# Up projection of forty column pairs as seven half-size products each, down projection as two sweeps over eight banks

## The chip, the cores and the metric

One core of a Trainium2 chip runs the whole program. The metric is device time in microseconds (us) of one execution. Five engines work side by side, each through its own queue in order: TensorE (PE; PEld is its weight load), VectorE (DVE), ScalarE (ACT), GpSimd (POOL) and SyncE (SP), which issues the DMAs. SBUF is the on-chip memory of 128 partitions, PSUM has eight banks of 128 x 512 float32, into which PE accumulates.

## What is computed

A decoder block for 512 tokens of width 2048: modulated RMS norm, a mixer, a residual, a second modulated norm, and the gated MLP that this case is about, with D_FF = 5632:

```python
h = _rmsnorm(x, norm2_g[l]) * (1.0 + sc2) + sh2
x = x + gt2 * _conv_ffn(h, w_up[l], conv_w[l], conv_b[l], w_down[l])
...
u = h @ w_up
up = jnp.pad(u, ((0, 0), (CONV_WIDTH - 1, 0), (0, 0)))
y = conv_b
for j in range(CONV_WIDTH):
    y = y + conv_w[j] * up[:, j:j + T]
val, gate = jnp.split(y, 2, axis=-1)
return (jax.nn.silu(gate) * val) @ w_down
```

The convolution runs over tokens, three taps per column. A final RMS norm ends the program. Everything is float32.

## The kernel before, in words

Activations lie transposed, columns on partitions and the 512 tokens along the free axis. A matrix product of float32 accuracy is made of three matmuls: weights and activations are each split into a high part (a cast to fp32r on ACT) and a low part (the rest, a subtraction on DVE), and `mm3` (L115 to L118) issues high x high (L116), high weights x low activations (L117) and low x high (L118). `split_weights` (L105 to L113) loads 128 x 512 weights into `wraw` (four buffers), casts them to `whi` on ACT (L110) and subtracts to `wlo` (L112, on DVE, or on POOL where a caller says so); `whi` and `wlo` have three buffers each. `project` runs a column tile's k-tiles through it, four at a time.

The program has a first part up to about 815 us (gates, input projection, mixers) that the change leaves as it is. Then, in the pool `rb`:

- The output projection, with the residual `x2` in 16 SBUF tiles and the sum of squares for the second norm. Its last columns are made by token halves, so that the norm of one half can begin early.
- `second_norm` (L144 to L146) writes the MLP's input H2, 16 tiles in high and low parts. `up_first` makes the first four column tiles by token halves, 256 tokens at a time, 16 k-tiles each; in the pass of the first half every other low part is made on POOL.
- A pair is the value tile j and the gate tile j, 44 pairs in all. `up_tile` makes one tile with 48 matmuls of 512 columns; `conv` applies the three taps (ACT at L896, DVE at L897 and L898, all of which read the bank), ACT does the Silu (L908), DVE the product (L909), and `split_act` the split into high and low (L138, L139).
- Pairs come in six groups (8, 8, 8, 8, 4, 8). After each group its part of the down projection runs: for each of the 16 output tiles the group's k-tiles into one bank, added to `x2` under the gate by DVE at L924. The last group does the final residual, the norm and the stores, its last eight tiles by token halves.
- `ada_gate2` computes the MLP's output gate, which needs 64 loads of 256 KB and 64 operations of DVE (L886); they are put behind pairs 4 to 7.

The order within an engine's queue is set by a scheduler with its own estimates of durations, from the order in which the code is written and from the buffers; queues are not reordered at run time.

## Time and profile before

| | |
|---|---|
| median of 3 runs | 2382.52 us (2381.91 to 2382.76) |
| the profiled execution's own time | 2381.72 us |
| its span in the trace | 2379.9 us |
| mean granted clock of PE | 0.979 |
| DVE busy, ACT busy, POOL busy | 1354.4 us, 821.2 us, 27.1 us |
| DMA | 357.06 MB, mean 150 GB/s |
| up-projection weights, down-projection weights | 368 and 192 loads of 256 KB |

The page gives, for each engine, its busy time, the chain of work that ended last, and groups of instructions by line with the mean duration of one and the idle time before them. Matmuls are pipelined, so the duration drawn for one is longer than the distance to the next; the distance is what counts. Lines are those of the program above, with L in front.

### The profile page before, as it was taken

Reading aid. Unit: us, or ns where it says so; the run is one execution under the profiler, and the core shown is the slowest. Engines: PE = TensorE matmul, PEld = TensorE weight load, DVE = VectorE, ACT = ScalarE, POOL = GpSimd, SP = SyncE. Lnnn points to the kernel's source line nnn. Section 1 sums busy time; section 2 is a strip of 40 time slices with the busy share of each in tenths; the row PEclk is TensorE's granted clock in tenths of the full one; section 3 lists DMA queues with packets and bytes.
Section 4 is the critical chain, followed back from the end, with each engine's and each line's share of the span. In section 5 each row is a group of like instructions: output and inputs, shape, how many; then the busy total and the mean of one; then the engine's idle time right before and its main releaser. Section 6 shows DMA issues by size and latency. Waiting matters only on the chain.

```text
span 2379.9 us, 36912 instructions
## 1 busy us (share of the span) xinstructions
PE 2258.0 (95%) x14434; PEld 1828.4 (77%) x14434; DVE 1354.4 (57%) x2258; ACT 821.2 (35%) x1361; POOL 27.1 (1%) x30
## 2 busy tenths in 40 slices
PE   7998898899879899999999999999999999999997
PEld 5776656666566799877888888888888888888886
DVE  7897767575875467577344433444344434444457
...
GB/s 350 296 301 168 171 178 182 185 124 215 219 232 149 182 173 207 104 224 223 97 97 96 96 98 98 98 98 94 97 97 98 98 97 97 95 97 98 98 101 174
DMA packets 188226, 357.06 MB, mean 150 GB/s; under 512 B 36497, under 2 KB 48529, under 8 KB 183825
## 3 DMA queue, kind: packets, MB, share of 16 engines
...
q8 instruction: 113, 1.85, 0.3%
...
HBM read 336.25 MB, written 18.36 MB: 149 GB/s over the span
## 4 chain that ended last, share of the span: by engine, by line
PE 76%; DMA 11%; DVE 7%; issue 3%; ACT 2%; SPq 1%; DVEq 0%; POOL 0%; ACTq 0%
PE b L116 20%; PE b L118 20%; PE b L117 20%; DMA war<-ada 4%; PE mm L118 2%; PE mm L117 2%; PE mm L116 2%; PE pf L116 2%; PE pf L118 2%; PE pf L117 2%; DMA wa<-ada 1%; DVE war L367 1%; DMA slot<-ada 1%; DVE wlo L112 1%; DMA wraw<-wup 1%
## 5 line engine op out<-in xcount | busy, mean ns | idle before, releaser
L112 DVE TENSOR_TENSOR wlo<-wraw,whi 128x512 fp32r<-128x512 f32 (+1 forms) x786 | 534.6, 682 | 664.8 <-ACT whi L110 650.1
L110 ACT CAST whi<-wraw 128x512 fp32r<-128x512 f32 (+1 forms) x802 | 490.9, 614 | 1222.2 <-PE b L117 918.4
L118 PE MATMUL b<-hh,wlo 128*128 128x512 f32 (+1 forms) x1472 | 560.9, 381 | 5.8 <-DVE wlo L112 5.5
L116 PE MATMUL b<-hh,whi 128*128 128x512 f32 (+1 forms) x1472 | 560.0, 380 | 0.8 <-ACT whi L110 0.8
L117 PE MATMUL b<-hl,whi 128*128 128x512 f32 (+1 forms) x1472 | 559.5, 380 | 0.0
L116 PE MATMUL b<-ah,whi 128*128 128x512 f32 (+1 forms) x980 | 350.3, 358 | 5.2 <-ACT whi L110 3.7
L118 PE MATMUL b<-ah,wlo 128*128 128x512 f32 (+1 forms) x980 | 349.3, 357 | 4.2 <-DVE wlo L112 4.2
L117 PE MATMUL b<-al,whi 128*128 128x512 f32 (+1 forms) x980 | 348.9, 356 | 0.0
L118 PEld LDWEIGHTS b<-hh,wlo 128*128 128x128 f32 x1472 | 277.0, 188 | 61.8 <-DVE wlo L112 8.2
L116 PEld LDWEIGHTS b<-hh,whi 128*128 128x128 f32 x1472 | 276.9, 188 | 53.1 <-ACT whi L110 1.4
L117 PEld LDWEIGHTS b<-hl,whi 128*128 128x128 f32 x1472 | 276.9, 188 | 52.7
L116 PEld LDWEIGHTS b<-ah,whi 128*128 128x128 f32 x980 | 186.4, 190 | 34.9 <-ACT whi L110 6.1
L118 PEld LDWEIGHTS b<-ah,wlo 128*128 128x128 f32 x980 | 186.3, 190 | 31.1 <-DVE wlo L112 5.3
L117 PEld LDWEIGHTS b<-al,whi 128*128 128x128 f32 x980 | 186.4, 190 | 26.8 <-DVE al L139 1.2
L118 PE MATMUL mm<-ah,wlo 128*128 128x512 f32 x444 | 187.6, 423 | 5.9 <-DVE wlo L112 5.8
L116 PE MATMUL mm<-ah,whi 128*128 128x512 f32 x444 | 186.6, 420 | 6.4 <-ACT whi L110 6.3
L117 PE MATMUL mm<-al,whi 128*128 128x512 f32 x444 | 184.9, 416 | 0.0
L367 DVE SCALAR_TENSOR_TENSOR war<-war,cq 128x1024 f32<-128x1024 f32 x96 | 117.2, 1222 | 83.2 <-DMA war<-ada 82.5
L924 DVE SCALAR_TENSOR_TENSOR x<-b,mod,x 128x512 f32<-128x512 f32 x80 | 59.7, 750 | 111.7 <-PE b L118 111.7
L116 PE MATMUL pf<-ah,whi 128*128 128x512 f32 x256 | 95.9, 404 | 20.6 <-ACT ah L214 19.5
L116 PEld LDWEIGHTS mm<-ah,whi 128*128 128x128 f32 x444 | 87.4, 197 | 32.0 <-ACT whi L110 8.1
L118 PEld LDWEIGHTS mm<-ah,wlo 128*128 128x128 f32 x444 | 87.2, 196 | 30.2 <-DVE wlo L112 8.4
...
## 6 DMA issues: line engine op xcount, KB each, us to landing
wraw<-wup SPq DMA_DIRECT2D x368, 256.0 KB, 3.0
...
wraw<-wdn SPq DMA_DIRECT2D x192, 256.0 KB, 2.7
...
```

What stands on the lines that cost most here:

```text
L110: S.copy(hi[:, 0:w], raw[:, 0:w])
L112: eng.tensor_tensor(lo[:, 0:w], raw[:, 0:w], hi[:, 0:w].bitcast(F32), op=ALU.subtract)
L116: PE.matmul(ps, wh, xh, start=start, stop=False)
L117: PE.matmul(ps, wh, xl, start=False, stop=False)
L118: return PE.matmul(ps, wl, xh, start=False, stop=stop)
L367: V.scalar_tensor_tensor(wa, wa, 1.0, cq[0], op0=ALU.mult, op1=ALU.mult, accum_out=modq[:, kq, j : j + 1])
L924: V.scalar_tensor_tensor(x2[f], ps, mod[:, 80 + f : 81 + f], x2[f], op0=ALU.mult, op1=ALU.add)
```

## The change

Pairs 0 to 3 stay as they were. For pairs 4 to 43 a pair's product is seen as a 2 x 2 block product: two halves of the 16 k-tiles by (gate, value) columns, times two halves of the tokens. It is computed with seven products of half the k-tiles and half the tokens in place of eight, from sums of weight quarters and sums of token quarters. The token sums are made once, on POOL (`token_sums`), cast on ACT and split on DVE, and lie in the slots `ah`, `al`. The weight sums are made per pair in four chunks (`seven`): one load of 512 KB brings four quarters of two k-tiles, POOL makes four sums, ACT and DVE split three quarters and four sums. The seven results stay in seven banks and are combined by ACT and DVE into `cv` and `cg`, in SBUF, which `conv` then reads. The packing of the weights on the host follows (`wups`), without arithmetic.

All 44 activation products are stored to DRAM (`actd`), and `x2` too (`x2d`). The down projection runs after all pairs, in two sweeps of eight output tiles, one bank each, over all 44 k-tiles in groups of four; the activations are loaded and split again in each sweep. The second sweep keeps its last eight k-tiles for the token halves. The loads and operations of `ada_gate2` are spread two to a pair over pairs 4 to 35.

```diff
-GROUPS = (8, 8, 8, 8, 4, 8)
+NORD = 4
+NPC = 4
+DK = 4
...
+    def gated(j, cv, cg):
+        yv, yg = conv(cv, j, "t0"), conv(cg, 44 + j, "t1")
+        S.activation(yg, yg, AF.Silu)
+        after = V.tensor_mul(yv, yv, yg)
+        nc.sync.dma_start(actd[j], yv)
+        return after
...
+    for j in range(2):
+        gated(j, ups[2 * j], ups[2 * j + 1])
...
+    def token_sums(i):
+        bb = up.tile([P, 2, T], F32, tag="raw", name="bb", bufs=3)
+        for q in range(2):
+            hi, lo = H2[i + HK * q]
+            G.tensor_tensor(bb[:, q, :], hi[:, :].bitcast(F32), lo[:, :].bitcast(F32), op=ALU.add)
+        tt = up.tile([P, 2, T], F32, tag="raw", name="tt", bufs=3)
+        t1, t2, t3, t4 = (tt[:, q // 2, (q % 2) * HT : (q % 2 + 1) * HT] for q in range(4))
+        G.tensor_tensor(t1, bb[:, 0, HT:], bb[:, 0, 0:HT], op=ALU.subtract)
+        G.tensor_tensor(t3, bb[:, 1, HT:], bb[:, 0, 0:HT], op=ALU.subtract)
+        G.tensor_tensor(t2, bb[:, 1, HT:], t1, op=ALU.subtract)
+        G.tensor_tensor(t4, t2, bb[:, 1, 0:HT], op=ALU.subtract)
+        got = []
+        for q in range(2):
+            hi, lo = slot(2 * i + q), slot(16 + 2 * i + q)
+            S.copy(hi, tt[:, q, :])
+            V.tensor_tensor(lo, tt[:, q, :], hi[:, :].bitcast(F32), op=ALU.subtract)
+            got += half([(hi, lo)], 0) + half([(hi, lo)], 1)
+        TK.append(got)
...
+    def seven(j):
+        q = {}
+        for c in range(NPC):
+            raw = up.tile([P, 4, W2], F32, tag="raw", name="raw", bufs=3)
+            nc.sync.dma_start(raw, a["wups"][j - NORD, c, :, :, :])
+            sm = [wp.tile([P, WC], F32, tag="wraw", name="sums", bufs=4) for _ in range(2)]
+            sa, sb2 = (t[:, :].rearrange("p (n w) -> p n w", n=2) for t in sm)
+            G.tensor_tensor(sa, raw[:, 1:3, :], raw[:, 0:1, :].to_broadcast([P, 2, W2]), op=ALU.add)
+            G.tensor_tensor(sb2[:, 0, :], sa[:, 0, :], raw[:, 2, :], op=ALU.add)
+            G.tensor_tensor(sb2[:, 1, :], sb2[:, 0, :], raw[:, 3, :], op=ALU.add)
...
+                    S.copy(hi[:, n : n + m, :], t)
+                    V.tensor_tensor(lo[:, n : n + m, :], t, hi[:, n : n + m, :].bitcast(F32), op=ALU.subtract)
...
+            a22, a11, a12 = parts([raw[:, 1:4, :]])
+            s1, s3, s2, s4 = parts([sa, sb2])
...
+            for n, w, xs_ in (
+                (1, a11, [x[0] for x in lo]), (2, a12, [x[1] for x in lo]),
+                (4, a22, [TK[k][3] for k in ks]), (6, s2, [TK[k][1] for k in ks]),
+                (7, s3, [TK[k][2] for k in ks]), (5, s1, [TK[k][0] for k in ks]),
+                (3, s4, [x[1] for x in hi]),
+            ):
...
+        S.copy(cg[:, A1], q[1])
+        V.tensor_tensor(cv[:, A1], cg[:, A1], q[2], op=ALU.add)
+        V.tensor_tensor(u[:, 0, :], cg[:, A1], q[6], op=ALU.subtract)
+        V.tensor_tensor(u[:, 1, :], u[:, 0, :], q[7], op=ALU.add)
+        V.tensor_tensor(u[:, 2, :], u[:, 0, :], q[5], op=ALU.subtract)
+        V.tensor_tensor(cg[:, B1], q[5], u[:, 1, :], op=ALU.subtract)
+        V.tensor_tensor(cv[:, B1], u[:, 2, :], q[3], op=ALU.add)
+        V.scalar_tensor_tensor(cg[:, A1], u[:, 1, :], -1.0, q[4], op0=ALU.mult, op1=ALU.subtract)
+        return cv, cg
...
+    for j in range(NORD, NF):
+        after = gated(j, *seven(j))
+        for n in range(2 * (j - NORD), 2 * (j - NORD + 1)):
+            if n < 4 * KT:
+                ada_gate2(n, after)
...
+    pss = [bank() for _ in range(NB)]
+    for k0 in range(0, NF, DK):
+        A = act_tiles(k0)
+        for f in range(NB):
+            down(pss[f], f, k0, DK, A, k0 == 0, k0 + DK == NF)
+            if k0 + DK == NF:
+                residual(f, pss[f], gate(f), acc, 0, T, f == 0)
```

Line numbers in the changed program: `mm3` L118 to L120, the casts and subtractions of `split_weights` L112 and L114; in `conv` and `gated` L833 to L835, L840 (Silu), L841 (product), L842 (store); the token sums L909 and L912 to L915 on POOL, L919 (cast) and L920 (subtraction); in `seven` L944 to L946 (POOL), L954 (cast), L955 (subtraction), L981 to L988 (the combination); L1002 the gate's operations.

Two places in the queues. The first is ACT at the end of `up_first`'s second pass and the start of the pairs (`whi` is a weight cast, `tk` a cast of a token sum `tt`; the number of a buffer rises with the program's order, and the casts up to whi_9739 before, whi_9818 now, are those of that pass). Before:

```order
L110 CAST whi_9703<-wraw_9701 128x512 [waits DMAHW3_49,DVE_49,PE_49]
L110 CAST whi_9721<-wraw_9719 128x512 [waits DMAHW4_49,DVE_49,PE_49]
L110 CAST whi_9739<-wraw_9737 128x512 [waits DMAHW5_49,DVE_49,PE_49]
L110 CAST whi_9795<-wraw_9793 128x512 [waits DMAHW6_49,DVE_49,PE_49]
L110 CAST whi_9813<-wraw_9811 128x512 [waits DMAHW7_49,DVE_49,PE_49]
L896 ACTIVATE t0_9764<-b_9084,vec_64 128x512 [waits PE_49]
```

With the change, from the eleventh token cast on:

```order
L919 CAST tk_9948<-tt_9943 128x512 [waits Pool_49]
L919 CAST tk_9952<-tt_9943 128x512 [waits Pool_49]
L112 CAST whi_9782<-wraw_9780 128x512 [waits DMAHW3_49,DVE_49,PE_49]
L919 CAST tk_9964<-tt_9959 128x512 [waits Pool_49]
L919 CAST tk_9968<-tt_9959 128x512 [waits Pool_49]
L112 CAST whi_9800<-wraw_9798 128x512 [waits DMAHW4_49,DVE_49,PE_49]
L919 CAST tk_9980<-tt_9975 128x512 [waits Pool_49]
L112 CAST whi_9818<-wraw_9816 128x512 [waits DMAHW5_49,DVE_49,PE_49]
L919 CAST tk_9984<-tt_9975 128x512 [waits Pool_49]
L112 CAST whi_9991<-wraw_9989 128x512 [waits DMAHW6_49,DVE_49,PE_49]
L112 CAST whi_10009<-wraw_10007 128x512 [waits DMAHW7_49,DVE_49,PE_49]
L833 ACTIVATE t0_9838<-b_9163,vec_64 128x512 [waits PE_49]
```

All 16 casts of token sums stand ahead of the first tap of pair 0, one or two between each two weight casts. Ahead of the first of them POOL has its 16 subtractions of `out_half` and `up_first`, and then the token sums, each dependent one with a wait:

```order
L114 TENSOR_TENSOR wlo_9532<-wraw_9528,whi_9530 128x512 [waits DVE_49,DMAHW5_49,PE_49,Activation_49]
L909 TENSOR_TENSOR bb_9860<-hh0_7868,hl0_7869 128x512
L909 TENSOR_TENSOR bb_9860<-hh8_7884,hl8_7885 128x512 [waits DVE_49]
L912 TENSOR_TENSOR tt_9863<-bb_9860 128x256 [waits Pool_49]
L913 TENSOR_TENSOR tt_9863<-bb_9860 128x256 [waits Pool_49]
L914 TENSOR_TENSOR tt_9863<-bb_9860,tt_9863 128x256 [waits Pool_49]
```

Before, POOL has nothing behind those 16 subtractions.

The second place is DVE in the steady part. Before, one pair of the fourth group (`t` is a tap's tile, `b` a bank):

```order
L897 SCALAR_TENSOR_TENSOR t_13901<-b,vec,t_13901 128x511
L898 SCALAR_TENSOR_TENSOR t_13901<-b,vec,t_13901 128x510
L112 TENSOR_TENSOR wlo<-wraw,whi 128x512 x4
L897 SCALAR_TENSOR_TENSOR t_13978<-b,vec,t_13978 128x511
L898 SCALAR_TENSOR_TENSOR t_13978<-b,vec,t_13978 128x510
L112 TENSOR_TENSOR wlo<-wraw,whi 128x512
L909 TENSOR_TENSOR t_13901<-t_13901,t_13978 128x512
L139 TENSOR_TENSOR al_13985<-t_13901,ah_13984 128x512
L112 TENSOR_TENSOR wlo<-wraw,whi 128x512 x3
```

With the change, the part of a pair in which the results of one pair are combined (`raw` a loaded quarter, `sums` POOL's sums, `ul` the low part, `cv`, `cg`, `u` the combination):

```order
L984 TENSOR_TENSOR u<-u,b 128x256
L985 TENSOR_TENSOR u<-u,b 128x256
L986 TENSOR_TENSOR cg<-b,u 128x256
L987 TENSOR_TENSOR cv<-u,b 128x256
L988 SCALAR_TENSOR_TENSOR cg<-u,b 128x256
L955 TENSOR_TENSOR ul<-raw,uh 128x768
L834 SCALAR_TENSOR_TENSOR t_11101<-cv,vec,t_11101 128x511
L834 SCALAR_TENSOR_TENSOR t_11105<-cg,vec,t_11105 128x511
L835 SCALAR_TENSOR_TENSOR t_11101<-cv,vec,t_11101 128x510
L835 SCALAR_TENSOR_TENSOR t_11105<-cg,vec,t_11105 128x510
L955 TENSOR_TENSOR ul<-sums,uh 128x512 x2
L841 TENSOR_TENSOR t_11101<-t_11101,t_11105 128x512
```

L982 and L983 stand ahead of these rows, each before a L955, and the two L1002 behind them. A pair has 26 operations on DVE now, 19 of them with all operands in SBUF and seven that read a bank, where it had 14; the taps read `cv` and `cg` in SBUF instead of a bank.

## Rows read from the trace of the kernel before

**Rows 1.** The page: busy times, and the chain that ended last by engine.
```profile
PE 2258.0 (95%) x14434; PEld 1828.4 (77%) x14434; DVE 1354.4 (57%) x2258; ACT 821.2 (35%) x1361; POOL 27.1 (1%) x30
...
PE 76%; DMA 11%; DVE 7%; issue 3%; ACT 2%; SPq 1%; DVEq 0%; POOL 0%; ACTq 0%
```

**Rows 2.** Stretches: us, busy PE, PEld, DVE, ACT, POOL (instructions), clock, DMA share, GB/s.
```profile
1000.00:1050.00 50.00, 49.64 (x220) 40.77 (x219) 32.40 (x67) 16.90 (x28) 0.00 (x0) 1.00 0.54 175
1050.00:1100.00 50.00, 45.17 (x188) 35.93 (x187) 39.34 (x95) 14.55 (x24) 0.00 (x0) 0.97 0.79 257
1100.00:2310.00 1210.00, 1210.00 (x5333) 999.83 (x5333) 531.05 (x786) 372.19 (x596) 0.00 (x0) 1.00 0.32 100
```

**Rows 3.** Timeline of PE in the tail: start, duration, first and last of 84.
```profile
2329.82 0.28 PE L116 MATMUL b<-ah,whi 128*128 128x256 f32 x1
...
2339.78 0.28 PE L118 MATMUL b<-ah,wlo 128*128 128x256 f32 x1
```

**Rows 4.** Groups of DVE from 860 us: count, busy us, mean ns, idle before.
```profile
L112 DVE TENSOR_TENSOR wlo<-wraw,whi 128x512 fp32r<-128x512 f32 x572 | 395.8, 693 | 586.8 <-ACT whi L110 582.5 <-PE b L117 1.1
...
L924 DVE SCALAR_TENSOR_TENSOR x<-b,mod,x 128x512 f32<-128x512 f32 x80 | 59.7, 750 | 111.7 <-PE b L118 111.7
L886 DVE SCALAR_TENSOR_TENSOR slot<-slot 128x512 f32<-128x512 f32 x64 | 42.3, 687 | 9.7 <-DMA slot<-ada 9.5
...
L144 DVE SCALAR_TENSOR_TENSOR h<-x,gsc,b 128x256 f32<-128x256 f32 x32 | 14.1, 469 | 0.0
...
L798 DVE SCALAR_TENSOR_TENSOR x<-b,mod,x 128x256 f32<-128x256 f32 x24 | 11.6, 484 | 6.8 <-PE b L118 6.3
```

**Rows 5.** Groups of ACT from 860 us.
```profile
L110 ACT CAST whi<-wraw 128x512 fp32r<-128x512 f32 x588 | 365.7, 623 | 945.1 <-PE b L117 899.6 <-DMA wraw<-wup 21.0 <-DMA wraw<-wdn 6.9
L896 ACT ACTIVATE t<-b,vec 128x512 f32<-128x512 f32 x88 | 67.8, 774 | 0.0
```

**Rows 6.** Timeline of DVE at 881 to 930, and at 1042.
```profile
881.84 0.86 DVE L144 SCALAR_TENSOR_TENSOR h<-x,gsc,b 128x256 f32<-128x256 f32 x2
...
886.54 0.48 DVE L798 SCALAR_TENSOR_TENSOR x<-b,mod,x 128x256 f32<-128x256 f32 x1 [0.27 <-PE b L118]
887.12 1.08 DVE L112 TENSOR_TENSOR wlo<-wraw,whi 128x512 fp32r<-128x512 f32 x1
...
928.40 0.48 DVE L146 SCALAR_TENSOR_TENSOR hl<-h,mod,hh 128x256 fp32r<-128x256 f32 x1
...
929.58 1.00 DVE L112 TENSOR_TENSOR wlo<-wraw,whi 128x512 fp32r<-128x512 f32 x1
...
1042.31 1.89 DVE L112 TENSOR_TENSOR wlo<-wraw,whi 128x512 fp32r<-128x512 f32 x3
```

**Rows 7.** Timeline of POOL at the same times.
```profile
886.34 1.30 POOL L112 TENSOR_TENSOR wlo<-wraw,whi 128x512 fp32r<-128x512 f32 x1 [2.21 <-DVE hl L146]
...
928.60 1.43 POOL L112 TENSOR_TENSOR wlo<-wraw,whi 128x512 fp32r<-128x512 f32 x1 [3.38 <-ACT whi L110]
```

**Rows 8.** Groups of POOL, whole span.
```profile
L112 POOL TENSOR_TENSOR wlo<-wraw,whi 128x512 fp32r<-128x512 f32 x16 | 21.0, 1310 | 304.5 <-ACT whi L110 293.8 <-DVE hl L146 8.8 <-DVE acc L791 1.9
...
L90 POOL MEMSET eps<- 128x1 f32 x1 | 0.1, 98 | 0.0
```

**Rows 9.** Timeline of ACT at the end of `up_first`'s second pass.
```profile
951.79 0.62 ACT L110 CAST whi<-wraw 128x512 fp32r<-128x512 f32 x1 [0.82 <-PE b L117]
953.23 0.62 ACT L110 CAST whi<-wraw 128x512 fp32r<-128x512 f32 x1 [0.82 <-PE b L117]
953.76 2.78 ACT L896 ACTIVATE t<-b,vec 128x512 f32<-128x512 f32 x4
```

**Rows 10.** One stretch of the first part, columns as in group 2.
```profile
820.00:840.00 20.00, 14.71 (x72) 12.16 (x71) 14.59 (x24) 9.15 (x16) 0.00 (x0) 0.74 0.71 243
```

More of the change, by code (lines that the diff above doesn't have):

```diff
@@ L776, in block_kernel, with stage @@
     HT = T // 2
+    H2 = [(rb.tile([P, T], F32R, tag=f"hh{k}", name=f"hh{k}"), rb.tile([P, T], F32R, tag=f"hl{k}", name=f"hl{k}"))
+          for k in range(KT)]
+    x2d = [tc.dram_tile([P, T], F32, name=f"x2d{f}") for f in range(KT)]
+    actd = [tc.dram_tile([P, T], F32, name=f"actd{j}") for j in range(NF)]
+    def stage(name):
+        st = ExitStack()
+        return st, st.enter_context(tc.tile_pool(name=name, bufs=1, reuse_waits="tile"))
     def bank():
@@ L865, in block_kernel @@
         up_first(1, k)
+    rxctx.close()
     if stop == "B":
         return
[L870 to L887 removed]
+    upctx, up = stage("up")
@@ L889, in up_tile @@
+    for i in range(HK):
+        token_sums(i)
     def up_tile(n):
         ps = bank()
[L891 removed]
+        project(ps, a["wup"][n - 4, :, :], H2)
         return ps
[L894 to L899 removed]
@@ new lines, in block_kernel, with ada_gate2 @@
+    cbs = []
+    modg = cp.tile([P, 4, KT], F32, tag="modg", name="modg")
+    def ada_gate2(n, after):
+        kq, j = divmod(n, KT)
+        if j == 0:
+            cbs.append(wp.tile([P, WC], F32, tag="whi", name="cb2", bufs=3))
+            nc.sync.dma_start(cbs[kq], cact[0:1, kq * T : (kq + 1) * T].partition_broadcast(P))
+        wa = wp.tile([P, WC], F32, tag="wlo", name="wa3", bufs=3)
+        nc.sync.dma_start(wa, a["ada3"][kq, j, :, :])
+        with tc.issue_after(after.ins):
+            V.scalar_tensor_tensor(wa, wa, 1.0, cbs[kq], op0=ALU.mult, op1=ALU.mult, accum_out=modg[:, kq, j : j + 1])
@@ new lines, in block_kernel, with gate, act_tiles @@
+    x2 = []
+    for f in range(KT):
+        t = rx.tile([P, T], F32, tag=f"x2_{f}", name=f"x2_{f}")
+        nc.sync.dma_start(t, x2d[f])
+        x2.append(t)
+    acc = rx.tile([P, T], F32, tag="acc", name="acc")
+    def gate(f):
+        return mod[:, 80 + f : 81 + f]
+    def act_tiles(k0):
+        got = []
+        for k in range(k0, k0 + DK):
+            t = wp.tile([P, WC], F32, tag="wraw", name="ald", bufs=4)
+            nc.sync.dma_start(t, actd[k])
+            got.append(split_act(k % KT, t))
+        return got
@@ new lines, in block_kernel @@
+    pss = [bank() for _ in range(NB)]
+    KL = NF - 2 * DK
+    for k0 in range(0, KL, DK):
+        A = act_tiles(k0)
+        for f in range(NB):
+            down(pss[f], NB + f, k0, DK, A, k0 == 0, k0 + DK == KL)
+            if k0 + DK == KL:
+                V.scalar_tensor_tensor(x2[NB + f], pss[f], gate(NB + f), x2[NB + f], op0=ALU.mult, op1=ALU.add)
+    A = act_tiles(KL) + act_tiles(KL + DK)
+    for hf in range(2):
+        for n in range(NB):
+            f = NB + n
+            if hf and n == 1:
+                dg = norm_rows(acc[:, 0:HT])
+            if hf and n == 2:
+                rstd = norm_bcast(dg)
+            if hf:
+                for k in range(max(3 * (n - 2), 0), min(3 * (n - 1), KT) if n < 7 else KT):
+                    finish(0, k, rstd)
+            ps = bank()[:, 0:HT]
+            down(ps, f, KL, 2 * DK, half(A, hf), True, True)
+            residual(f, ps, gate(f), acc, hf * HT, (hf + 1) * HT, False)
@@ L964, in pack @@
+    rstd = norm_bcast(norm_rows(acc[:, HT:T]))
+    for k in range(KT):
+        finish(1, k, rstd)
+    rxctx.close()
 def pack(x, c, w_ada, b_ada, norm1_g, w_in, mu_shift, w0, w2, a0, a2, g2, k_k, k_a, r_k, ln_x_w, ln_x_b,
```

149 lines of the change are left out of this document (61 added, 88 removed).

## The prediction

> **What bounds the kernel now.** I read the page first: TensorE is busy for 95% of the span and 76% of the chain that ended last is PE, in the three lines of `mm3` [rows 1]. Then the table of stretches [rows 2]: from 1100 to 2310 us PE is never idle, at a granted clock of 1.00, while DVE is busy for 531 of 1210 us, ACT for 372 and POOL for none. So in the stage that the change rewrites PE alone sets the time, and 1210.00 us / 5333 matmuls = 0.2269 us per 512-column matmul. The only hole of that stage is at 1050 to 1100, 50 - 45.17 = 4.8 us (and 0.4 before it), where the 64 loads of the second adaLN gate fall into five pairs and DMA stands at 0.79. Anything that the change saves must therefore be PE issue time, and anything that it adds to DVE, ACT or POOL is free only as long as these stay below PE's own time for a pair.
>
> **PE's side of the change.** A pair is now 96 matmuls of 512 columns, 96 x 0.2269 = 21.78 us; 40 pairs are 871.3 us. Seven half-size products are 7 x 8 k-tiles x 3 = 168 matmuls of 256 columns. Their price stands in the tail of this kernel: from 2329.82 to 2339.78 there are 83 steps of one 256-column matmul, 9.96 / 83 = 0.120 us each [rows 3], although each is drawn 0.28 us long. 168 x 0.120 = 20.16 us, 806.4 us for 40 pairs: **64.9 us less**, if the weights come in time.
>
> **DVE's side, per pair.** Back to back, three 512-element subtractions take 1.89 us where one takes 0.68, so each further one costs 0.605; two 256-element ones take 0.86 with 0.47 for one, a pitch of 0.39 [rows 4, 6]. A 768-element one is then 0.605 + 0.215 = 0.82. The new queue of a pair is 4 x 0.82 + 8 x 0.605 (L955) + 4 taps x 0.62 (L834, L835, by the same shape of L886) + 0.605 (L841) + 2 x 0.62 (L1002) + 7 x 0.42 (L982 to L988, which read a bank; between the pitch 0.39 and the 0.48 of L798) = 15.4 us. That alone is under 20.16. ACT: four casts of 768 at about 0.83, eight of 512 at 0.62, two taps at 0.77 [rows 5], one Silu and one copy make about 11 us. It is hidden by PE's 20.16 us; without that cover it would still be the shorter queue.
>
> **POOL's side.** Nothing in the steady part runs on POOL today; what it costs there has to come from the 16 subtractions it makes near 880 to 930, 1.30 us for 512 elements [rows 7, 8]. For 256 elements there is no row: without any fixed part 0.65, all fixed 1.30; I take 0.70, with the 0.10 us of a one-element memset as the fixed part [rows 8], since that is the nearest row to a POOL instruction without work. Per pair 4 x 1.30 + 8 x 0.70 = 10.8 us.
>
> These are not beside DVE's work. While POOL runs from 886.34 to 887.64, DVE's L798, which reads a bank, takes its usual 0.48 us; but L112 with two SBUF operands, issued at 887.12, takes 1.08 instead of 0.68 and ends 0.56 after POOL. At 928.40 DVE is first: it ends at 928.88, POOL ends 1.15 later (1.43 instead of 1.30), and the next L112 ends 0.55 after that [rows 6, 7]. So the two exclude each other, and a 512-element POOL operation between two such DVE operations puts 1.15 + 0.55 = 1.70 us where 0.605 stood: it adds 1.10, which is its 1.30 less 0.20. For 256 elements I take 0.70 - 0.20 = 0.50 (bounds 0.45 and 1.10). A pair adds 4 x 1.10 + 8 x 0.50 = 8.4 us, of which the five bank-reading operations in a row (L984 to L988, 2.1 us) hide one of each size, 1.6, and the two that stand singly about 0.35 each: 6.1 us is left.
>
> DVE's queue of a pair is then 15.4 + 6.1 = **21.5 us, more than PE's 20.16**; the bound moves from PE to DVE with POOL. The last eight pairs have no L1002: 21.5 - 1.24 = 20.3. Sum: 32 x 21.5 + 8 x 20.3 = 850.4 us against 871.3: **-20.9 us** (bounds: -64.9 if nothing collides; with 256 elements at 1.10 each pair is 4.8 longer, +171, an end that I don't weigh since it needs an operation of half the size to cost the same).
>
> The page SBUF — State Buffer of the Trainium skill, section "SBUF: two separate sides", says that the port pair shared by VectorE and GpSimd is an exclusive lock, held for the whole instruction, and that the loser blocks fully. That the loser blocks the rows above show; that POOL's whole instruction counts they don't quite (1.10 of 1.30). Taken to the letter it gives the second rival below.
>
> **The start of the seven.** The token sums are the dearest single step. POOL's last subtraction of the stage before ends at 930.03 [rows 7]; only then come the 48 operations of the eight `token_sums`, 16 x 1.30 + 32 x 0.70 = 43.2 us, of which all but L909 wait for POOL's own result. ACT's queue of the change has the 16 casts of their results (L919, each waiting for POOL) between the weight casts of the second `up_first` pass, and DVE's has L920 between the subtractions; both are in order. That pass now ends at 953.76, where ACT's L896 finds its banks done [rows 9]; it uses a weight cast every 1.44 us. With the change its 16th cast stands behind the cast of the last-but-one token result. POOL: 930.0 + 43.2 + about 1 for hand-overs + 9 for DVE's 34 operations in between (at most 34 x (0.55 - 0.15) = 13.6) = 983.2; less the last sum 0.7, plus two casts, a subtraction and 12 matmuls, 3.4: 985.9. **+32 us** that PE stands idle and nothing gives back, since PE is in order (bounds: +23 with no DVE operation in the way, +51 with 256 elements at 1.30). While it idles the granted clock may fall, as in 820 to 840, where PE was busy for 14.71 of 20 us at 0.74 [rows 10]: +2 (0 to 5).
>
> **The rest.** The gate's loads are now two a pair: the hole of 5.2 us goes, -5.2 (bound 0, if PE waits there for something else). Down projection: the number of matmuls is the same. The 80 operations of L924, 59.7 us, go, but they waited 111.7 us for PE and delayed nobody [rows 4]: 0. Each activation tile is split twice, from DRAM: twelve DVE operations in a group of four tiles, 7.3 us beside 8 x 12 x 0.2269 = 21.8 us of PE: 0; were PE not there, 7.3 us a group. The 16 stores and loads of x2 and the 44 stores and 88 loads of activations, 256 KB each, go through SP, at a DMA share of 0.32 in that stage [rows 2]: 0. In the steady part SP's store of a pair (L842) waits for L841 with two gate loads and the next weight quarters behind it; the weights have three buffers, about three quarters of a pair ahead: 0. At the passage to the down projection the last two of the first four activation loads wait for buffers that the last sums free, then load, cast and subtract before PE can go on: +3 (0 to 8). The final halves are as before.
>
> **Sum:** -20.9 + 32 + 2 + 3 - 5.2 = +10.9 us on the profiled execution's 2381.7, 2392.6; the median of the runs lies 0.8 above it: **2393.5 us**. Its own range is 2365 to 2425 (0.5 us a pair either way is 20 us; the start -9 to +19).
>
> **Rival 1, faster: PE still binds.** Decided in DVE's queue of a pair: if POOL's twelve operations leave less than 20.16 - 15.4 = 4.8 us there instead of 6.1, the pair costs 20.2 and 40 of them save 63 us. For it: much of DVE's queue waits for PE's results anyway, and POOL may run in those gaps; 1.3 us is little. Against it: a queue that binds has no such gaps. Time: -63 + 32 + 2 + 3 - 5.2 = -31 us, 2351.
>
> **Rival 2, slower: the whole POOL instruction counts.** Then a pair adds 10.8 us less all 2.9 us of bank-reading operations, 7.9: 23.3 us a pair and 22.1 in the last eight, 922 us, +51; in the start each DVE operation delays POOL by its 0.605, 20.6 instead of 9, so +44. Together +95: 2477. For it: operations that depend on each other on POOL may have gaps between them that I count as nothing. Against it: the 1.70 us measured for one of each. This is the rule of the page named above, as a time.
>
> That the seven products are not what they seem is no rival: the order shows 168 matmuls of 256 columns in a pair.
>
> **How the numbers follow.** Forecast 0.63, rival 1 0.22, rival 2 0.15. About 0.2%, 4.8 us, is what a measurement of this kernel can tell from no change; of the forecast's range about 0.38 lies above that, 0.10 within and 0.15 below. Faster 0.22 + 0.15 = 0.37, same 0.10, slower 0.38 + 0.15 = 0.53. The range reaches down to rival 1 and up past the forecast's own end, 2348 to 2450, and leaves out rival 2 and some of the edges.
>
> **What would show it.** Right: PE idle for some 30 us between 930 and 990 behind ACT's whi, that behind POOL; in the steady part POOL at about half busy, L955 of 512 elements at a mean well above 0.68 us, PE at 92 to 95%, with its idle time released by DVE's ul; the last eight pairs shorter than the others by a us. Wrong: PE at 100% in the pairs (rival 1), 23 us a pair (rival 2), a second `up_first` pass that ends near 954, or PE waiting for DMA or for banks rather than for ul.

## The result

The changed kernel takes 2408.95 us (median of 4 runs, 2405.55 to 2411.78) where the kernel before takes 2382.64 on the same chip: **slower by 1.06%, ratio 1.0106, 95% interval 1.0088 to 1.0124**, some 26 us. The forecast was 2393.5, with a range of 2348 to 2450. The side was right and the range held the time, but the loss is 2.4 times the 10.9 us of the sum. (In the diff above, L913 of the token sums is misprinted: its second operand is `bb[:, 0, HT:]`.)

The page of the changed kernel, busy times and the chain that ended last; its span is 2409.9 us:

```profile
PE 2212.3 (92%) x17314; PEld 1923.0 (80%) x17314; DVE 1791.8 (74%) x2686; ACT 984.0 (41%) x1621; POOL 768.8 (32%) x558
...
PE 69%; DVE 13%; DMA 10%; issue 3%; ACT 2%; POOL 2%; SPq 1%; DVEq 0%; ACTq 0%; POOLq 0%
```

Against [rows 1] PE's share of the chain fell from 76 to 69% and DVE's rose from 7 to 13%. Where this happens is in the table of stretches, with the columns of [rows 2]:

```profile
950.00:1000.00 50.00, 30.60 (x146) 26.03 (x145) 36.32 (x36) 18.22 (x32) 41.41 (x37) 0.69 0.28 88
...
1200.00:1400.00 200.00, 188.18 (x1542) 185.65 (x1541) 200.00 (x259) 92.13 (x146) 158.99 (x112) 1.00 0.41 137
...
1800.00:1900.00 100.00, 98.01 (x808) 96.99 (x807) 83.26 (x114) 49.59 (x80) 79.19 (x53) 1.00 0.33 114
...
2000.00:2350.00 350.00, 349.84 (x1567) 290.43 (x1566) 150.17 (x222) 126.13 (x206) 0.00 (x0) 1.00 0.50 148
```

In the middle of the pairs DVE is busy for all of 200 us and PE for 94% of them: the bound has moved from PE to DVE. In the last eight pairs, 1800 to 1900, DVE is busy for 83% and PE for 98%: there PE is the bound but for one short wait a pair, shown below. The down projection is PE again. From 950 to 1000 PE works for 30.6 of 50 us, at a granted clock of 0.69.

To place the 30.0 us between the two spans (that of the changed kernel is the longest of its four executions) I cut both traces at three marks: PE's wait for the last residual of the stage ahead (810.37 before, 812.06 now), the first output projection matmul after the hole that follows it (827.96, now 835.56), and the first tap of pair 0 (953.76 in [rows 9], now 994.89).

| stretch | before | changed | difference | forecast |
|---|---|---|---|---|
| up to the first mark, not touched by the change | 810.4 | 812.1 | +1.7 | 0 |
| to the output projection | 17.6 | 23.5 | +5.9 | 0 |
| to the first tap | 125.8 | 159.3 | +33.5 | +34 (32 and 2 for the clock) |
| to the end: pairs and down projection | 1426.1 | 1415.0 | -11.1 | -23.1 |

So the dearest single step came out as forecast; a cost that I had put at nothing came in ahead of it; and the gain in the pairs and behind them is half of what I had worked out.

**The hole before the output projection.** SP's timeline of the changed kernel, then PE's, and last the same two rows before the change:

```profile
814.79 4.69 SPq L850 DMA_DIRECT2D x<-part  x10
819.53 4.20 SPq L850 DMA_DIRECT2D x<-xT  x6
824.30 5.77 SPq L856 DMA_DIRECT2D x2d<-x  x8
830.24 7.70 SPq L110 DMA_DIRECT2D wraw<-wout  x7
```

```profile
835.56 0.80 PE L118 MATMUL b<-ah,whi 128*128 128x512 f32 x1 [7.61 <-ACT whi L112]
```

```profile
822.39 27.47 SPq L108 DMA_DIRECT2D wraw<-wout  x19
...
827.96 0.80 PE L116 MATMUL b<-ah,whi 128*128 128x512 f32 x1 [1.90 <-ACT whi L110]
```

Eight of the new stores of x2 stand in SP's queue between the loads of x and the weight loads, and hold the queue for 5.77 us. Before, the weight loads begin 12.0 us after the first mark (822.39); now 18.2 us after it (830.24). It is not DVE that the stores wait for: seven of their eight residuals had ended by 824.88, just after the first store was issued, and 3.0 us of SP's waits at the stores are put down to the landing of the loads of x ahead of them. PE names ACT's cast as what it waited for; that cast itself waited 5.64 us for the DMA of its weights.

**The start of the seven.** POOL's first token operation and its last, and ACT between its last two weight casts of `up_first` and the first tap:

```profile
936.45 3.17 POOL L909 TENSOR_TENSOR bb<-hh,hl 128x512 f32<-128x512 f32 x2
...
992.32 0.72 POOL L915 TENSOR_TENSOR tt<-tt,bb 128x256 f32<-128x256 f32 x1
```

```profile
985.58 0.62 ACT L919 CAST tk<-tt 128x512 fp32r<-128x512 f32 x1 [4.74 <-POOL tt L914]
986.39 0.62 ACT L919 CAST tk<-tt 128x512 fp32r<-128x512 f32 x1 [0.19 <-POOL tt L915]
986.92 0.61 ACT L112 CAST whi<-wraw 128x512 fp32r<-128x512 f32 x1
992.27 0.62 ACT L919 CAST tk<-tt 128x512 fp32r<-128x512 f32 x1 [4.74 <-POOL tt L914]
992.79 0.62 ACT L112 CAST whi<-wraw 128x512 fp32r<-128x512 f32 x1
993.32 0.61 ACT L919 CAST tk<-tt 128x512 fp32r<-128x512 f32 x1
993.84 1.13 ACT L112 CAST whi<-wraw 128x512 fp32r<-128x512 f32 x2
994.89 1.45 ACT L833 ACTIVATE t<-b,vec 128x512 f32<-128x512 f32 x2
```

The weight cast at 992.79 follows the one before it after 5.87 us, where in [rows 9] it was 1.44. ACT is idle 4.74 us ahead of each of these pairs of token casts, for POOL, and the weights of PE's next 12 matmuls stand behind them. DVE's queue has the same order, its subtraction of a token cast ahead of that of a weight, so PE is drawn waiting for both: from 930 to 995 for 16.0 us on DVE's `wlo` and 8.4 us on ACT's `whi`. POOL's 48 operations take from 936.45 to 993.04, 56.6 us, where 53.2 were forecast. A 256-element operation that nothing disturbs is 0.72 us, as taken (0.70).

**The pairs.** The first tap of four pairs on ACT, two in the middle and two of the last eight:

```profile
1128.15 0.81 ACT L833 ACTIVATE t<-cv,vec 128x512 f32<-128x512 f32 x1 [0.71 <-DVE cv L987]
...
1149.86 0.82 ACT L833 ACTIVATE t<-cv,vec 128x512 f32<-128x512 f32 x1 [0.71 <-DVE cv L987]
...
1799.19 0.82 ACT L833 ACTIVATE t<-cv,vec 128x512 f32<-128x512 f32 x1 [0.90 <-DVE cv L987]
...
1819.99 0.81 ACT L833 ACTIVATE t<-cv,vec 128x512 f32<-128x512 f32 x1 [0.89 <-DVE cv L987]
```

A pair takes 21.7 us (forecast 21.5), one of the last eight 20.8 (forecast 20.3). DVE's costliest groups from 1100 to 1780 (count, busy us, mean ns, idle before):

```profile
L955 DVE TENSOR_TENSOR ul<-sums,uh 128x512 fp32r<-128x512 f32 x251 | 227.3, 934 | 1.8 <-ACT uh L954 1.7
L955 DVE TENSOR_TENSOR ul<-raw,uh 128x768 fp32r<-128x768 f32 x126 | 208.2, 1652 | 1.5 <-ACT uh L954 1.5
L1002 DVE SCALAR_TENSOR_TENSOR wa<-wa,cb 128x512 f32<-128x512 f32 x60 | 71.4, 1224 | 0.0
L834 DVE SCALAR_TENSOR_TENSOR t<-cv,vec,t 128x511 f32<-128x511 f32 x32 | 39.2, 1224 | 0.0
...
L835 DVE SCALAR_TENSOR_TENSOR t<-cv,vec,t 128x510 f32<-128x510 f32 x31 | 22.8, 737 | 0.0
...
L986 DVE TENSOR_TENSOR cg<-b,u 128x256 f32<-128x256 f32 x32 | 13.1, 409 | 0.0
```

L955 of 512 elements has a mean of 934 ns and not 680, the 768-element one 1652; L986, which reads a bank, has its 409. All the long operations have their operands in SBUF, and none that reads a bank is long: that is the exclusion that the prediction read from [rows 6, 7]. Not every operation in SBUF is long: L835 has its 737, and POOL stands idle for 119.1 us in all in this stretch, waiting for DVE's `ul`.

**The last eight pairs.** PE at the wait of one of them, and one L955 of 768 elements on DVE in the middle and one here:

```profile
1846.32 0.28 PE L119 MATMUL b<-tk,uh 128*128 128x256 f32 x1
1847.00 0.39 PE L120 MATMUL b<-tk,ul 128*128 128x256 f32 x1 [0.40 <-DVE ul L955]
1847.22 0.28 PE L118 MATMUL b<-tk,uh 128*128 128x256 f32 x1
```

```profile
1422.08 2.04 DVE L955 TENSOR_TENSOR ul<-raw,uh 128x768 fp32r<-128x768 f32 x1
...
1847.47 0.94 DVE L955 TENSOR_TENSOR ul<-raw,uh 128x768 fp32r<-128x768 f32 x1
```

Two steps of PE take 0.68 and 0.22 us where the pitch is 0.12, 0.66 us more; 168 matmuls at 0.120 are 20.16 us, and with this wait 20.82; the taps are 20.80 apart. DVE is busy for 83.26 of 100 us, 17.3 us a pair and not the 20.3 of the forecast. POOL makes the same twelve sums as in the other pairs, but here they lengthen DVE's operations by only 3.2 us a pair: the means from 1800 to 1883 are 1004 ns for L955 of 768 elements, 938 for 512 and 1224 for the two L834, where they are 952, 687 and 750 without POOL (next section).

### The profile page after: what moved, and what is told of

Read it like the earlier page. It is cut to its first block, busy times and chain, and to the rows that moved or that the text cites. A ratio compares the mean times of both kernels' runs of the same rounds, so it can differ in the third digit from the quotient of the medians.

```text
span 2409.9 us, 44500 instructions
## 1 busy us (share of the span) xinstructions
PE 2212.3 (92%) x17314; PEld 1923.0 (80%) x17314; DVE 1791.8 (74%) x2686; ACT 984.0 (41%) x1621; POOL 768.8 (32%) x558
## 4 chain that ended last, share of the span: by engine, by line
PE 69%; DVE 13%; DMA 10%; issue 3%; ACT 2%; POOL 2%; SPq 1%; DVEq 0%; ACTq 0%; POOLq 0%
PE b L120 18%; PE b L118 17%; PE b L119 17%; DMA war<-ada 5%; DVE ul L955 3%; PE mm L120 3%; PE mm L118 3%; PE mm L119 3%; PE pf L118 2%; PE pf L119 2%; PE pf L120 2%; DVE wlo L114 1%; DVE war L369 1%; DVE t L834 1%; POOL bb L909 1%
## 5 line engine op out<-in xcount | busy, mean ns | idle before, releaser
L114 DVE TENSOR_TENSOR wlo<-wraw,whi 128x512 fp32r<-128x512 f32 (+1 forms) x466 | 324.8, 699 | 317.7 <-ACT whi L112 309.4
L112 ACT CAST whi<-wraw 128x512 fp32r<-128x512 f32 (+1 forms) x482 | 290.8, 606 | 562.4 <-PE b L119 255.2
L944 POOL TENSOR_TENSOR sums<-raw 128x512 f32<-128x512 f32 x160 | 324.4, 2028 | 185.0 <-DVE ul L955 151.1
L120 PE MATMUL b<-tk,ul 128*128 128x256 f32 x1280 | 366.0, 286 | 2.6 <-DVE ul L955 2.6
L118 PE MATMUL b<-ah,whi 128*128 128x512 f32 (+1 forms) x980 | 350.3, 357 | 14.6 <-ACT whi L112 13.6
L118 PE MATMUL b<-tk,uh 128*128 128x256 f32 x1280 | 362.1, 283 | 0.0
L119 PE MATMUL b<-tk,uh 128*128 128x256 f32 x1280 | 362.0, 283 | 0.0
L120 PE MATMUL b<-ah,wlo 128*128 128x512 f32 (+1 forms) x980 | 349.5, 357 | 5.6 <-DVE wlo L114 4.7
L120 PE MATMUL b<-hh,ul 128*128 128x256 f32 x960 | 274.9, 286 | 37.4 <-DVE ul L955 37.4
L955 DVE TENSOR_TENSOR ul<-sums,uh 128x512 fp32r<-128x512 f32 x320 | 288.9, 930 | 18.2 <-ACT uh L954 17.4
L118 PE MATMUL b<-hh,uh 128*128 128x256 f32 x960 | 271.6, 283 | 0.0
L119 PE MATMUL b<-hl,uh 128*128 128x256 f32 x960 | 271.5, 283 | 0.0
L955 DVE TENSOR_TENSOR ul<-raw,uh 128x768 fp32r<-128x768 f32 x160 | 246.5, 1541 | 13.3 <-ACT uh L954 13.2
L120 PEld LDWEIGHTS b<-tk,ul 128*128 128x128 f32 x1280 | 245.3, 192 | 5.8 <-DVE ul L955 4.2
L118 PEld LDWEIGHTS b<-tk,uh 128*128 128x128 f32 x1280 | 245.5, 192 | 0.0
L119 PEld LDWEIGHTS b<-tk,uh 128*128 128x128 f32 x1280 | 245.4, 192 | 0.0
L954 ACT CAST uh<-sums 128x512 fp32r<-128x512 f32 x320 | 182.7, 616 | 148.2 <-PE b L119 133.3
L118 PEld LDWEIGHTS b<-ah,whi 128*128 128x128 f32 x980 | 186.2, 190 | 43.0 <-ACT whi L112 17.1
L120 PEld LDWEIGHTS b<-hh,ul 128*128 128x128 f32 x960 | 184.0, 192 | 43.9 <-DVE ul L955 43.9
L120 PEld LDWEIGHTS b<-ah,wlo 128*128 128x128 f32 x980 | 186.1, 190 | 33.6 <-DVE wlo L114 6.6
L954 ACT CAST uh<-raw 128x768 fp32r<-128x768 f32 x160 | 132.8, 830 | 193.0 <-PE b L119 193.0
```

The lines of the kernel that those rows point to most:

```text
L112: S.copy(hi[:, 0:w], raw[:, 0:w])
L114: eng.tensor_tensor(lo[:, 0:w], raw[:, 0:w], hi[:, 0:w].bitcast(F32), op=ALU.subtract)
L118: PE.matmul(ps, wh, xh, start=start, stop=False)
L119: PE.matmul(ps, wh, xl, start=False, stop=False)
L120: return PE.matmul(ps, wl, xh, start=False, stop=stop)
L944: G.tensor_tensor(sa, raw[:, 1:3, :], raw[:, 0:1, :].to_broadcast([P, 2, W2]), op=ALU.add)
```

## The experiments

Two theories stood against each other in each: the account above (called A in the expectations), by which DVE's queue, ACT's queue and SP's queue each cost a part of their own, and a rival (B) that explains the same rows otherwise. Ratios are to the kernel before on the same chip; the changed kernel has 1.0106. A difference from the changed kernel is one of the two times; by the ratios it is 2 to 4 us smaller, as the kernel before had 2382.64 us beside the changed kernel and 2379.0 to 2382.2 beside the edits.

### Weight sums on DVE

```diff
-            G.tensor_tensor(sa, raw[:, 1:3, :], raw[:, 0:1, :].to_broadcast([P, 2, W2]), op=ALU.add)
+            V.tensor_tensor(sa, raw[:, 1:3, :], raw[:, 0:1, :].to_broadcast([P, 2, W2]), op=ALU.add)
...
```

(and L945, L946 likewise)

> The changed kernel with the twelve weight sums of a pair (L944 to L946) on DVE instead of POOL, nothing else. Theory A (VectorE and GpSimd exclude each other, and DVE's queue, lengthened by that, sets the 21.70 us of a pair): without POOL the 26 operations fall back to about 15.4 us, the sums add 4 x 0.605 + 8 x 0.39 = 5.5 us, so 20.9 us a pair in 32 pairs and at most the 20.8 of now in the last eight: 25 us less than the changed kernel, about 2384 us; L955 of 512 elements returns from 0.93 to 0.65 us. Theory B (the DVE operations of this shape and type simply take that long, and POOL's work runs beside them for nothing): the sums come on top, 21.7 + 5.5 = 27.2 us a pair, 200 us more, about 2610 us.

Measured: 2366.24 us, ratio 0.994 (0.992 to 0.996): faster than the kernel before. DVE's groups in the same stretch:

```profile
L955 DVE TENSOR_TENSOR ul<-sums,uh 128x512 fp32r<-128x512 f32 x266 | 182.3, 687 | 3.1 <-ACT uh L954 0.9
L955 DVE TENSOR_TENSOR ul<-raw,uh 128x768 fp32r<-128x768 f32 x133 | 126.6, 952 | 0.0
L944 DVE TENSOR_TENSOR sums<-raw 128x512 f32<-128x512 f32 x132 | 90.5, 685 | 0.0
...
L1002 DVE SCALAR_TENSOR_TENSOR wa<-wa,cb 128x512 f32<-128x512 f32 x60 | 38.9, 686 | 0.0
L834 DVE SCALAR_TENSOR_TENSOR t<-cv,vec,t 128x511 f32<-128x511 f32 x34 | 25.5, 750 | 0.2 <-ACT t L833 0.2
```

All are back at their own durations. Per pair the difference of the means is 4 x 0.70 + 8 x 0.247 + 2 x 0.54 + 0.47 = 6.3 us: that is what POOL's twelve operations took from DVE in the pairs that have gate operations, and the prediction had 6.1. A pair with gate operations takes 20.53 us (the first taps of 30 of them lie between 1118.91 and 1714.25), with DVE busy for 199.22 of 200 us, and one of the last eight 20.16; over all 40 it is 20.45. The gain is 1.17 us in 32 pairs and 0.65 in the last eight, together the 42.7 us between the two times; my 0.8 was too low because DVE's queue is 20.5 us and not 20.9. With 15.4 for the rest, the same sums done on DVE itself cost about 5 us.

### The same, and POOL makes the sums once more for nobody

```diff
+            G.tensor_tensor(dm, raw[:, 1:3, :], raw[:, 0:1, :].to_broadcast([P, 2, W2]), op=ALU.add)
+            G.tensor_tensor(dm[:, 0, :], dm[:, 0, :], raw[:, 2, :], op=ALU.add)
+            G.tensor_tensor(dm[:, 1, :], dm[:, 0, :], raw[:, 3, :], op=ALU.add)
```

> As e1_sums_dve (weight sums on DVE, 20.45 us a pair), and POOL makes the same twelve operations a pair once more into a tile that nothing reads. Theory A (each POOL operation shuts DVE out for its time less 0.2 us): DVE's queue of 20.3 us gets 4 x 1.10 + 8 x 0.52 = 8.6 us, less up to 2.3 behind the operations that read a bank: 26.6 to 28.9 us a pair, 250 to 340 us over e1_sums_dve, 2610 to 2710 us. Theory B (the pairs of the changed kernel are long because DVE or ACT waits for POOL's results): no one waits for these, so the time stays at 2366 us.

Measured, in one profiled execution: 2654.38 us. The first taps lie between 1061.0 and 2143.6 for 40 pairs, 27.8 us a pair, 7.3 more than without. Nobody waits for these results. There is still a wait for POOL: `dm` takes one of the three `wlo` slots, and SP's loads for the gate stand 101.9 us in all, from 1200 to 1600, for POOL to leave one. But in that stretch, at 28.1 us a pair, DVE is idle for only 1.1 us a pair, so some 6.5 of the 7.6 us over 20.53 are DVE's longer operations: the exclusion.

```profile
1200.00:1600.00 400.00, 327.14 (x2384) 315.76 (x2383) 384.08 (x573) 146.04 (x227) 198.05 (x169) 0.92 0.33 104
```

POOL is busy for half of that stretch, DVE for 96%, and PE, with the same matmuls as before, for 82%, at a granted clock of 0.92.

### Token casts behind the Silu of pairs 1 to 4

```diff
-NORD = 4
+NORD = 6
...
-            S.copy(hi, tt[:, q, :])
+            with tc.issue_after(silu[-1].ins):
+                S.copy(hi, tt[:, q, :])
...
-    for i in range(HK):
-        token_sums(i)
...
     for j in range(2, NORD):
+        for i in (2 * j - 4, 2 * j - 3):
+            token_sums(i)
```

> The changed kernel with two more pairs made the old way (pairs 4 and 5) and the casts of the token sums put behind the Silu of pairs 1 to 4, two tokens a pair; POOL's work is the same. Theory A (PE stands in the second up_first pass because its weight casts stand behind token casts in ACT's in-order queue): the pass ends as before the change, the first tap comes about 35 us earlier, two pairs cost 21.78 instead of 21.70; about 2374 us. Theory B (the start is lost because POOL's and DVE's work collide in the ports, wherever the casts stand, or because the seven's own first loads are late): POOL's 57 us are only moved, PE waits at the first seven instead, and the time stays within 10 us of the changed kernel's 2409.

Measured: 2385.99 us, ratio 1.0016 (1.0000 to 1.0032): 23 us less than the changed kernel, not 35. ACT at the end of the second `up_first` pass:

```profile
958.65 0.62 ACT L112 CAST whi<-wraw 128x512 fp32r<-128x512 f32 x1 [0.82 <-PE b L119]
960.09 0.62 ACT L112 CAST whi<-wraw 128x512 fp32r<-128x512 f32 x1 [0.82 <-PE b L119]
960.61 2.79 ACT L833 ACTIVATE t<-b,vec 128x512 f32<-128x512 f32 x4
```

The casts are 1.44 us apart again, as in [rows 9], and wait for PE, not for POOL. From the first mark (807.67 here) to the first tap are 152.9 us instead of 182.8: 30 us of the 33.5 are gone. The edit moves more than the casts, though: a token's sums need a buffer that the casts ahead of them free, so POOL stands idle for 21.47 us from 948.65 on and makes 34 of its 48 token operations only from 970.12 on, beside the old pairs. The 30 us are the price of the casts and of those sums in that place together. About 3.6 stay, with DVE's second norm stretched by POOL between 900 and 950 (PE busy for 45.23 us; 48.18 in the kernel below that has the token sums on DVE). Of the 30 some 5 are lost again in pairs 2 to 5 (PE busy for 46.92 us of 1000 to 1050): the load of the first weight quarters waits 7.4 us for POOL's last token sum to leave a buffer, ACT's cast of them waits for that load, and a weight cast behind it is late for PE by 2.1 us.

### The x2 stores later

```diff
-        nc.sync.dma_start(x2d[f], x2[f])
...
-        if hf:
-            nc.sync.dma_start(x2d[f], x2[f])
...
     for k in range(KT):
+        nc.sync.dma_start(x2d[k], x2[k])
         up_first(1, k)
```

> The changed kernel with the 16 stores of x2 written later in the code, beside the second up_first pass, so that in SP's queue at most two stand between weight loads instead of eight ahead of the loads. Theory A (the hole of PE at 828 to 836 us is SP waiting at the stores, each for DVE's residual, with the weight loads behind them): the hole shrinks by about 6 us; 2403 us. Theory B (the hole is DMA traffic, 0.97 busy at 815 to 830, so that stores or loads take as long in any order): no change, 2408 to 2410 us.

Measured: 2400.96 us, ratio 1.0084 (1.0064 to 1.0105). The interval overlaps that of the changed kernel, so the time alone does not settle it; the trace does. From the first mark (805.00) PE reaches the same matmul in 17.97 us instead of 23.50, its wait there 3.27 instead of 7.61:

```profile
817.46 2.36 SPq L110 DMA_DIRECT2D wraw<-wout  x4
820.11 0.33 SPq L887 DMA_DIRECT2D x2d<-x  x1
823.40 2.99 SPq L110 DMA_DIRECT2D wraw<-wout  x3
```

Four weight loads are ahead of the first store now. The next three stand behind it, but come no later: 5.94 us after the first, where before the change it was 6.27. So the order of the queue made the hole, as A has it, though not by waits for DVE.

### Old up projection, new down projection

```diff
-NORD = 4
+NORD = 44
...
-        after = gated(j, *seven(j))
+        after = gated(j, up_tile(2 * j), up_tile(2 * j + 1))
```

> Only the second half of the change: all 44 pairs made the old way, no token sums; activations and x2 through DRAM, the gate's operations two a pair, and the down projection in two sweeps. Theory A (down projection costs nothing but the 6 us of the x2 stores, about 5 us at the passage, and gains the 5 us of the gate's hole): 2382 + 6 + 5 - 5, about 2388 us, between 2382 and 2395. Theory B (loading and splitting the activations twice costs in the sweeps, or the sweeps with one bank for a tile gain something): outside of that range. Against the changed kernel it also gives the up projection's part alone: by the account of the trace it is +35 us at the start and -9 us in 40 pairs, +26.

Measured: 2422.34 us, ratio 1.0169 (1.0143 to 1.0195): outside the range of A, and not for the reasons of B. PE's waits in its trace (us in total, times, longest):

```profile
PE b L120 <- DVE wlo L114: 30.8, 71, 3.9
```

The gate's operations, two a pair, use the `wlo` buffers, which the old pairs need and the seven products leave idle. That is a reading; the next kernel tests it.

```diff
-        wa = wp.tile([P, WC], F32, tag="wlo", name="wa3", bufs=3)
+        wa = up.tile([P, WC], F32, tag="wa3", name="wa3", bufs=3)
```

(and the gate's other tile likewise)

> As e4_old_up (old up projection, new down projection), but the gate's loads and their operations get buffers of their own instead of the wlo and whi buffers of the weights. In e4_old_up PE waited 30.8 us in 71 places for DVE's wlo while these operations ran, two a pair, and none after them. Theory A (each gate load takes one of the three wlo buffers that the old pairs need, which the seven products do not use): the waits go, and what is left over the kernel before is the 6 us of the x2 stores and some us at the passage: 2385 to 2392 us. Theory B (the two operations a pair and their place behind the product of a pair delay DVE's own subtractions, whatever the buffer): it stays at 2415 to 2425 us.

Measured: 2375.08 us, ratio 0.9977 (0.9962 to 0.9993).

```profile
PE b L120 <- DVE wlo L114: 6.9, 7, 3.7
```

24 us of drawn waits are gone and 47 us of time. The drawn idle time is too little, since the long bars of pipelined matmuls cover short waits: from 1100 to 1200 PE made 419 matmuls with the shared buffers and 443 with own ones, 5.4 us less work, of which 2.9 were drawn as idle. What remains says that the down projection in two sweeps, with x2 and the activations through DRAM, costs nothing against the kernel before: with the gate's hole gone it is 2 to 9 us better by the interval, although PE's wait behind the stores of x2 is in this kernel too (7.4 us at that place). All of the loss, and more, comes with the up projection.

### Gate operations in the down projection

```diff
-        wa = wp.tile([P, WC], F32, tag="wlo", name="wa3", bufs=3)
+        wa = rb.tile([P, WC], F32, tag=f"hh{n % 8}", name="wa3")
...
-        for n in range(2 * (j - NORD), 2 * (j - NORD + 1)):
-            if n < 4 * KT:
-                ada_gate2(n, after)
...
     for k0 in range(0, NF, DK):
         A = act_tiles(k0)
+        for n in range(7 * (k0 // DK), 7 * (k0 // DK) + 7):
+            if n < 4 * KT:
+                ada_gate2(n, None)
```

> The changed kernel with the 64 gate operations (L1002) and their loads moved out of the pairs into the first sweep of the down projection, in the buffers of H2, which are free by then. Theory A (DVE's queue, stretched by POOL, sets the pair): a pair loses two operations and about half a POOL collision, 21.70 to 20.8, as in the last eight pairs now, 32 x 0.9 = 29 us less, about 2380 us; DVE in the sweeps has room. Theory B (PE or POOL sets the pair, or DVE's time is only traded): under 8 us less, and the loads come back as waits in the sweep.

Measured: 2393.95 us, ratio 1.0060 (1.0037 to 1.0082): about 15 us less (11 by the ratios), half of the expectation or less. A pair is at the 20.8 that was expected (168 matmuls a pair, 1615 of them in 200 us), with DVE busy for 168.64 of 200 us: without the two gate operations DVE no longer sets the pair, and they gave back 4 us of DVE's time, not 1.24:

```profile
1200.00:1400.00 200.00, 195.97 (x1615) 193.95 (x1614) 168.64 (x233) 98.23 (x155) 168.60 (x114) 1.00 0.35 114
...
1850.00:1900.00 50.00, 43.71 (x225) 36.23 (x224) 36.73 (x74) 17.64 (x29) 5.88 (x3) 0.90 0.85 285
1900.00:1950.00 50.00, 48.07 (x206) 37.58 (x204) 33.60 (x82) 15.48 (x26) 0.00 (x0) 1.00 0.87 282
1950.00:2000.00 50.00, 45.91 (x193) 35.73 (x194) 29.93 (x70) 14.71 (x25) 0.00 (x0) 1.00 0.75 238
```

The rest is lost at the passage, where the gate's loads meet those of x2, the activations and the first weights, at a DMA share of 0.75 to 0.87: PE works for 137.7 of 150 us.

### The edits together

The first is the four edits: sums on DVE, casts spread, x2 stores late, gate operations in the sweep.

> All four edits together: weight sums on DVE, token casts behind pairs 1 to 4 (with two more old pairs), x2 stores late, gate operations in the down projection. Theory A (the three terms are separate: DVE's queue in the pairs, ACT's queue at the start, SP's queue before it): PE sets the pair at 20.2 to 20.4, 38 pairs; against the changed kernel -50 in the pairs, -23 for the token casts, -5 for the stores: about 2332 us, 2 per cent under the kernel before. Theory B (one of them only uncovers the next wait, for example DMA or ACT in the pairs): not under 2350.

Measured: 2347.65 us, ratio 0.9854 (0.9832 to 0.9877), 1.5% under the kernel before. PE sets the pair; the passage (1800 to 1950) and the start take back what was missing to 2332. The second adds this, and the token sums on DVE (`G` to `V` in `token_sums`):

```diff
-        nc.sync.dma_start(wa, a["ada3"][kq, j, :, :])
+        with tc.issue_after(after.ins):
+            nc.sync.dma_start(wa, a["ada3"][kq, j, :, :])
```

(`after` is the group's last activation load)

> As e7_all, with two edits more: the gate's loads in the first sweep stand behind the activation loads of their group, seven a group, instead of at its start, where e7_all had DMA at 0.80 and PE short of 14 us between 1800 and 1950; and the token sums on DVE, whose operations of the second norm POOL's stretched at 900 to 950 (PE 42.4 of 50 us). Theory A (both losses are collisions in time, and go when the work is spread): 10 us less at the passage and 4 at the start, about 2334 us. Theory B (the passage is lost to the last pair's combination and to x2's loads, the start to the token work on whatever engine): 2345 to 2352 us, as e7_all.

Measured: **2333.67 us, ratio 0.9793 (0.9771 to 0.9816)**, 2.1% faster than the kernel before and the best of this study.

```profile
900.00:950.00 50.00, 48.18 (x396) 47.51 (x395) 45.59 (x90) 29.31 (x57) 12.04 (x9) 1.00 0.61 183
...
1100.00:1700.00 600.00, 600.00 (x5003) 600.00 (x5002) 577.72 (x1073) 304.15 (x477) 0.00 (x0) 1.00 0.35 118
...
1800.00:1850.00 50.00, 37.33 (x171) 30.10 (x171) 28.00 (x61) 14.27 (x25) 0.00 (x0) 0.90 0.81 274
```

The start is nearly free of idle time. A pair takes 600 / 5003 x 168 = 20.15 us, PE's price from [rows 3], which the changed kernel never reached. The passage still loses 12.7 us. A last kernel spread the 16 loads of x2 as well, and moved the gate's loads to the eight groups behind the first, eight a group:

```diff
-        nc.sync.dma_start(t, x2d[f])
...
+        if 1 <= g <= NB:
+            load_x2(g - 1)
+        for n in range(8 * (g - 1), 8 * g):
+            if 0 <= n < 4 * KT:
+                ada_gate2(n, lds[-1])
```

(and eight more loads of x2 in the second sweep)

> As e8_paced, with the 16 loads of x2 spread too, one a group over both sweeps, and nothing but weights and activations in the first group of the first sweep. In e8_paced DMA is busy for 0.81 between 1800 and 1850 and PE for 37.3 of 50 us there. Theory A (x2's and the gate's loads stand ahead of the first weights of the sweep): most of these 12.7 us go, about 2323 us. Theory B (PE waits at the passage for the last pairs' taps, Silu and product, whose store and load back come before the last group, or for banks): no change, 2330 to 2337 us.

Measured: 2340.33 us, ratio 0.9832 (0.9808 to 0.9855), not better. From 1800 to 1850 PE works for 45.96 us now, but the loss has moved: 1850 to 1900 has 46.35, 1900 to 2000 has 91.54 of 100. In total 16 us are lost between 1800 and 2000, where the kernel ahead of it loses 17. So A is right about the first 50 us, where 8.6 of the 12.7 us went, and wrong about the time; B's time is nearly right, without its reason. What costs PE those 16 us is not shown. That the gate's and x2's loads stand ahead of weights in SP's queue wherever they are put is a guess; they were not tried on another queue.

## Why the prediction came out as it did

**Right in the mechanism, for 32 of the 40 pairs.** PE does not bind these pairs any more; DVE does, with POOL's exclusion in its queue. The sum 15.4 + 6.1 = 21.5 us became 21.70, and the lengthening by itself was 6.3. The 15.4 is borne out by the last eight pairs: 17.3 us of DVE less 3.2 of lengthening is 14.1, and 15.4 less the 1.24 of the gate operations is 14.2. Rival 1, in which POOL fits into gaps, falls here: DVE has no gap in 200 us. Rival 2, in which a whole POOL instruction counts, falls too: 23.3 us a pair were not seen. Of POOL's 11 us a pair only 6.3 reached DVE's queue; the operations that read a bank kept their durations beside it.

The Trainium skill, page SBUF — State Buffer, section "SBUF: two separate sides", says that the loser of the shared port blocks fully. The trace agrees for the operation that is in the way (a 768-element L955 at 1652 against 952 ns).

**Partly luck in the 6.1.** It was worked out as one price for POOL's twelve operations, and the same price was put on the last eight pairs, where 3.2 was measured. A POOL operation that comes between DVE operations standing close together can also wait itself: the sum at 1846.42 takes 4.36 us while four DVE operations in SBUF run at their own durations. So what POOL takes depends on how the two queues meet, and how much of this the gate operations decide is not shown.

**Right in size, in part by luck.** "The start of the seven", +32 and +2 for the clock: 33.5. The chain was the one described, POOL ahead of the token casts ahead of the weight casts, and the experiment with the casts and most of the sums elsewhere gave 30 of it back. Inside it POOL's 48 operations took 56.6 us and not 53.2, while the first tap came 1.9 us behind them and not 2.7, and they began 1.2 us earlier against the output projection than forecast. The 2 us for the clock cannot be seen by themselves, though the granted clock did fall, to 0.69 from 950 to 1000.

**The steps that failed.** Three, all to the same side:

- "The 16 stores and loads of x2 ... go through SP, at a DMA share of 0.32 in that stage [rows 2]: 0." It was 5.9 us. I looked at how busy the DMA engines are, in a stretch of the wrong stage (they were at 0.71 where the stores are [rows 10]), where the cost lies in the order of the queue: eight stores hold the weight loads behind them for 5.8 us, and 5.5 of the 5.9 went when they were moved. I had asked this question of the stores of the pairs, and not of these.
- "32 x 21.5 + 8 x 20.3". The 0.2 us by which 21.5 was short is 6.4 us in 32 pairs. In the last eight the bound itself was wrong: the formula had DVE at 20.3 us, but DVE's queue is 17.3, and PE binds at its 20.16 with 0.66 us a pair lost at the `ul` that stands behind the taps; 20.81 and not 20.3, 4.1 us. With both, the pairs gave 10.4 us and not 20.9.
- The rest (passage and gate) is 1.5 us worse than summed; which of the two failed is not shown. And 1.7 us of the difference of the two traces lies ahead of the first mark, where nothing was changed.

10.9 + 5.9 + 10.5 + 1.5 + 1.7, less 0.5 at the start, is 30.0, the difference of the spans. The forecast was a difference of two large terms, -20.9 and +34, so that errors of 10 and 6 us doubled it.
